# Order of filler work, of late products and of a few sums in a two-layer decoder kernel

## The chip, the cores and the metric

The kernel runs on one core of one Trainium2 chip. The metric is the time of one execution in microseconds (us). Three runs of the kernel before took 2700.45, 2702.9 and 2701.96 us, so the median is 2701.96 us.

The engines are named as the profile names them: PE is TensorE (matrix products, transposes), PEld its weight loads, DVE is VectorE, ACT is ScalarE, POOL is GpSimd, SP is SyncE, whose queue issues the transfers.

## The reference

Two layers run over 1024 tokens of 1024 features, all in fp32. Cut to what matters:

```python
for l in range(DEPTH):                       # 2
    h = rmsnorm(x, norm1[l])
    qa, ka, va, qb, kb, vb, gate_pre = jnp.split(h @ w_in[l], splits, axis=-1)
    o_a = dilated_mixture(qa, ka, va)        # 12 heads in 3 groups: window, dilation (128,1) (512,4) (2048,16)
    o_b = stick_breaking_attention(qb, kb, vb)   # 4 heads
    gates = sigmoid(gate_pre + b_gate[l]); g_a, g_b = gates[..., :D], gates[..., D:]
    x = x + (g_a * (o_a @ w_br[l, :256]) + g_b * (o_b @ w_br[l, 256:])) @ w_o[l]
    up = rmsnorm(x, norm2[l]) @ w_up[l]      # 1024 x 5632
    a, v = up[..., :2816], up[..., 2816:]
    a = causal_depthwise_conv(a, conv_w[l], conv_b[l])      # 3 taps
    x = x + (gelu(a) * v) @ w_down[l]
out = rmsnorm(x, norm_f)
```

Stick-breaking attention takes, for a query and the keys before it, the sigmoid of a score times the product of one minus the sigmoids of all keys between.

## The kernel before

**Arithmetic.** Each fp32 operand of a product is split in two parts, `hi` (a cast by ACT, L129) and `lo` (the rest, a subtraction by DVE, L130). A product is three matrix products: hi with hi, hi with lo, lo with hi (`product`, L150 to L159; `seven`, L902 to L909). Large products are cut into blocks of which seven, instead of eight, are multiplied; the sums and differences of blocks that this needs are made by POOL and DVE.

**Who sets the order.** PE runs in the order in which the program is written (L1870). ACT, DVE, POOL and SP are put in order by a planner: among the pieces that are ready on its own clock it takes the one written earliest. `tc.high_priority(offset=AHEAD)`, AHEAD being 200, lets pieces count as if they had been written 200 instructions earlier. While FFN units from the third on are written (L1714), ACT, DVE and POOL too run in the written order; SP does not.

**The mixer.** The attention is a list of 36 items (L1203 to L1216): 16 of stick-breaking attention (B00 to B17, line names `z`, `beta`, `sb_t`, `sb_o`), four of the near group (N00 to N11: `z0`, `p0`, `t0`, `o0`), 16 of the two far groups (T00 to T17: `z10`, `p1`, `t1`, `o1`). The trace leaves digits at the end of names out. An item has *scores* (PE products into a bank of PSUM, then DVE and ACT) and pairs of a *turn* (PE transposes of the weights, then a split by ACT and DVE in `parts`, L593) and a *product* with the values. PE does nothing else between them than *filler steps* of the dense projections: keys, queries, values, gates (`k_ps`, `q_ps`, `v_ps`, `r_ps`, `i_a`, `i_c`). A step is six matrix products. `attend` (L312) writes this order: the scores of the next item among the turns and products of this one, each product one place behind the next turn; the last product of an item (`late`) goes behind the first turn of the next. `Dense.step` (L254) writes one filler step. `Dense.advance(rate)` (L285) also lets one prepared piece of block sums go (`aside`), and adds the rate to an account, `due`; each whole unit in it buys a step. The rates are 0.68, 0.85, 0.88 and 0.77 (L41). If the next item is not ready when the current one begins, its scores are left over: `attend` then runs the dense units on until it is, two steps more, and then the scores.

**The queries** (`queries_half`, L532) of the second stick-breaking pair and of the near items: a product into a bank with the tag `ps`, of which there are two, then two multiplies by ACT (L538), two copying transfers from SP (L540), and two subtractions by DVE (L543, L544). Only after the last one can a later unit have the bank.

**The FFN.** A unit j makes 128 columns of the gate half and of the value half; `gated` (L1373) multiplies them. Units are taken in pairs, an even and an odd one, for the seven-product form of the down projection: `less` (L1381) makes differences on POOL (L1382), and `spill` (L1404) splits a block and writes it to DRAM (`gd`). `at(k, f)` runs f k steps later. `C[0]`, the two blocks of unit 0, lies in a buffer with the tag `ql`, of which there are two; the raw weights of a later unit (`up_a`, L1493 to L1495) take the same tag. The turn of unit 1 comes while units 2 and 3 run.

The lines that choose where fillers and late products go:

```python
for f in sc:                      # the first item's scores, L323
    f()
    dense.advance(rate)
...
if m == 0 and late:               # L331
    seq.append(late)
...
if nxt:                           # scores left over, L369
    for f in nxt:
        f()
        dense.advance(rate)
```

Of the kernel before, what the change touches and what calls it, by code (L numbers as in the profile page):

```python
# [11 lines left out]
ALU = mybir.AluOpType  # L12
# [32 lines left out]
AHEAD = 200  # L45
# [7 lines left out]
def trunk_kernel(ctx, tc, x, norm1, w_in, b_gate, w_br, w_o, norm2, w_up, conv_w, conv_b, w_down, norm_f, out, depth=None, probe=None):  # L53
# [258 lines left out]
    def attend(dense, items):  # L312

        late = None
        for i, (name, first, rest, rate, make) in enumerate(items):
            if i == 0:
                dense.until(first)
                dense.step()  # L320
                dense.step()
                sc, micro = make()
                for f in sc:  # L323
                    f()
                    dense.advance(rate)
                dense.done.add(name + "s")
            dense.until(rest)
            seq = []
            for m, (t, p) in enumerate(micro):
                seq.append(t)  # L330
                if m == 0 and late:  # L331
                    seq.append(late)
                if m >= 1:
                    seq.append(micro[m - 1][1])

            def late(f=micro[-1][1], name=name):
                f()
                dense.done.add(name)

            nxt, nmicro = [], None  # L340
            pending = items[i + 1] if i + 1 < len(items) else None

            def begin():
                nonlocal pending, nxt, nmicro
                if pending and set(pending[1]) <= dense.done:
                    nxt, nmicro = pending[4]()
                    pending = None

            begin()
            if pending or i + 1 == len(items):  # L350
                seq.append(late)
                late = None
            gap = max(1.0, len(seq) * 0.7 / max(1, len(nxt)))
            at = 0.0
            for j, f in enumerate(seq):
                if nxt and j >= at:
                    nxt.pop(0)()
                    at += gap
                    if not nxt:
                        dense.done.add(items[i + 1][0] + "s")  # L360
                    dense.advance(rate)
                f()
                dense.advance(rate)
            if pending:
                dense.until(pending[1])
                dense.step()
                dense.step()
                begin()
            if nxt:  # L369
                for f in nxt:  # L370
                    f()
                    dense.advance(rate)
                dense.done.add(items[i + 1][0] + "s")
            micro = nmicro

    H = [[None, None], [None, None]]

    def h_part(n, k):
        return H[n][0][:, k, :], H[n][1][:, k, :]
# [150 lines left out]
        yield  # L530

    def queries_half(q, w, n, scale, copies=False):  # L532
        qt, ql = q
        o = bank("ps", "q_ps")
        yield from product(o, [(w[k], h_part(n, k)) for k in range(KD)])
        qa, qb, la, lb = (a[:, i, n * HF : (n + 1) * HF] for a in (qt, ql) for i in range(2))
        for q2, src, mine, other in ((qa, o[0:64], slice(0, 64), slice(64, 128)), (qb, o[64:128], slice(64, 128), slice(0, 64))):
            act.mul(q2[mine], src, scale)  # L538
            if copies:
                nc.sync.dma_start(f32(q2[other]), f32(q2[mine]))  # L540
            else:
                act.mul(q2[other], src, scale)
        dve.scalar_tensor_tensor(la[0:64], o[0:64], scale, f32(qa[0:64]), ALU.mult, ALU.subtract)  # L543
        dve.scalar_tensor_tensor(lb[64:128], o[64:128], scale, f32(qb[64:128]), ALU.mult, ALU.subtract)  # L544
        yield

    def new_q():

# [773 lines left out]
    def ffn(l, pending, final):  # L1322
# [50 lines left out]
        def gated(j, n, v):  # L1373


            c = C[j][n]
            dve.tensor_tensor(c, c, v, ALU.mult)  # L1377

            later = (2, 3, 4, 5, 7) if j == 1 else (3, 5, 7, 9, 11) if j == NF - 1 else (1, 4, 7, 11, 14)

            def less(dst, a, b):  # L1381
                return lambda: pool.tensor_tensor(dst, a, b, ALU.subtract)  # L1382

            if j % 2 == 0:
                c11, c12 = C[j]
                if n == 0:
                    at(3, lambda: spill(j, 0, c11))
                else:
                    at(4, less(c11, c12, c11))
                    at(6, lambda: spill(j, 5, c11))  # L1390
            elif n == 1:
                s1, c12 = C[j - 1]
                c21 = C[j][0]
                at(1, less(c12, c, c12))
                at(1, less(s1, c, s1))
                at(later[0], lambda: spill(j, 6, c))
                at(later[1], lambda: spill(j, 2, c12))

                at(later[1], less(c, c21, s1))
                at(later[2], lambda: spill(j, 1, s1))  # L1400
                at(later[3], lambda: spill(j, 4, c21))
                at(later[4], lambda: spill(j, 3, c))

# [493 lines left out]
```

## Time and profile before

| what | value |
|---|---|
| median of three runs | 2701.96 us |
| the profiled execution | 2703.52 us, of which the span from the first to the last instruction is 2701.8 us |
| granted TensorE clock, mean | 0.996 |
| PE busy | 98% of the span |
| DVE busy | 78% |
| ACT busy | 49% |
| POOL busy | 27% |

Layer 1's mixer takes about 72 to 575 us of the span (B items to 230, N items to 330, T items from 397 to 556), its FFN starts at 735; layer 2's mixer takes about 1410 to 1912 us.

How to read the rows: in a list of waits a row says which engine's instruction (line, tile) sat idle until which other engine's piece was done, then the total in us, the number of times, and the longest. In a timeline a row has the start, the duration, the engine, the line, the operation, what it writes and reads, the shapes and a count, and in square brackets how long the engine stood idle in front of it and for whom. In a table of stretches each engine has its busy time and a count, then comes the granted clock, the DMA share and GB/s.

### The profile page before, as it was taken

Reading aid. Unit: us, or ns where it says so; the run is one execution under the profiler, and the core shown is the slowest. Engines: PE = TensorE matmul, PEld = TensorE weight load, DVE = VectorE, ACT = ScalarE, POOL = GpSimd, SP = SyncE. Lnnn points to the kernel's source line nnn. Section 1 sums busy time; section 2 is a strip of 40 time slices with the busy share of each in tenths; the row PEclk is TensorE's granted clock in tenths of the full one; section 3 lists DMA queues with packets and bytes.
Section 4 is the critical chain, followed back from the end, with each engine's and each line's share of the span. In section 5 each row is a group of like instructions: output and inputs, shape, how many; then the busy total and the mean of one; then the engine's idle time right before and its main releaser. Section 6 shows DMA issues by size and latency. Waiting matters only on the chain. (4 is left out here: it accounts for less than half of the span.)

```text
span 2701.8 us, 37158 instructions
## 1 busy us (share of the span) xinstructions
PE 2650.5 (98%) x13098; PEld 2226.4 (82%) x13098; DVE 2115.7 (78%) x3170; ACT 1314.3 (49%) x2434; POOL 734.9 (27%) x531
## 2 busy tenths in 40 slices
PE   8999999999999999999999999999999999999999
PEld 7888888888888888888889878888788888888888
DVE  5888876675789988897658887766858888998865
ACT  5656544364455555432335655434635555554225
POOL 2004133222233434321120042332311433343210
PEclk9999999999999999999999999999999999999999
DMA  4134489863235444688401334988732443447963
GB/s 153 28 97 125 132 239 234 205 229 118 82 117 172 141 156 143 222 325 313 167 32 48 102 120 145 254 208 226 234 90 75 151 160 135 170 144 254 333 246 121
DMA packets 399559, 448.88 MB, mean 166 GB/s; under 512 B 22044, under 2 KB 319372, under 8 KB 397836
## 3 DMA queue, kind: packets, MB, share of 16 engines
q1 hardware_dynamic: 399372, 446.49, 51.9%
q8 instruction: 104, 1.70, 0.3%
q14 instruction: 83, 0.68, 0.1%
HBM read 300.61 MB, written 142.67 MB: 164 GB/s over the span
## 5 line engine op out<-in xcount | busy, mean ns | idle before, releaser
L130 DVE TENSOR_TENSOR w_lo<-up_a,w_hi 128x512 fp32r<-128x512 f32 x240 | 236.9, 993 | 22.5 <-ACT w_hi L129 22.5
L129 ACT CAST w_hi<-up_a 128x512 fp32r<-128x512 f32 x240 | 149.4, 623 | 186.0 <-PE u_a L906 45.8
L1651 DVE TENSOR_TENSOR x<-x,d_ps 128x512 f32<-128x512 f32 (+1 forms) x228 | 152.3, 672 | 78.0 <-PE d_ps L1645 77.0
L1382 POOL TENSOR_TENSOR cv<-cv 128x512 f32<-128x512 f32 x88 | 131.9, 1509 | 249.0 <-DVE cv L1377 139.1
L130 DVE TENSOR_TENSOR w_lo<-w_raw,w_hi 128x512 fp32r<-128x512 f32 x176 | 133.9, 763 | 64.9 <-ACT w_hi L129 62.3
L129 ACT CAST w_hi<-w_raw 128x512 fp32r<-128x512 f32 x176 | 109.1, 621 | 130.1 <-PE o_ps L156 60.2
L129 ACT CAST w_hi<-in_a 128x512 fp32r<-128x512 f32 x140 | 86.8, 620 | 148.8 <-PE i_a L906 83.4
L130 DVE TENSOR_TENSOR g<-cv,g 128x512 fp32r<-128x512 f32 x154 | 152.3, 990 | 5.2 <-ACT g L129 2.8
L1643 PE MATMUL d_ps<-gd_in,w_hi 128*128 128x512 f32 (+1 forms) x340 | 130.2, 383 | 1.5 <-ACT w_hi L129 1.2
L1645 PE MATMUL d_ps<-gd_in,w_lo 128*128 128x512 f32 (+1 forms) x340 | 129.8, 382 | 0.0
L1644 PE MATMUL d_ps<-gd_in,w_hi 128*128 128x512 f32 (+1 forms) x340 | 129.7, 382 | 0.0
L905 PE MATMUL u_a<-hh,w_hi 128*128 128x512 f32 x320 | 124.7, 390 | 2.7 <-DVE u L1533 2.7
L906 PE MATMUL u_a<-t_lo,w_hi 128*128 128x512 f32 x320 | 124.5, 389 | 0.0
L907 PE MATMUL u_a<-hh,w_lo 128*128 128x512 f32 x320 | 124.5, 389 | 0.0
L905 PE MATMUL u_a<-t_hi,w_hi 128*128 128x512 f32 x320 | 124.5, 389 | 0.0
L906 PE MATMUL u_a<-hl,w_hi 128*128 128x512 f32 x320 | 124.5, 389 | 0.0
L907 PE MATMUL u_a<-t_hi,w_lo 128*128 128x512 f32 x320 | 124.5, 389 | 0.0
L130 DVE TENSOR_TENSOR w_lo<-in_a,w_hi 128x512 fp32r<-128x512 f32 x140 | 115.6, 826 | 3.8 <-ACT w_hi L129 3.5
L1038 POOL TENSOR_TENSOR in_a<-in_a 128x512 f32<-128x512 f32 x28 | 38.0, 1357 | 281.3 <-DVE w_lo L130 281.3
L1643 PE MATMUL d_ps<-gd_in,wd 128*128 128x512 f32 (+1 forms) x292 | 113.9, 390 | 0.0
L129 ACT CAST g<-cv 128x512 fp32r<-128x512 f32 x154 | 94.9, 616 | 38.1 <-POOL cv L1382 29.3
L1645 PE MATMUL d_ps<-gd_in,wd 128*128 128x512 f32 (+1 forms) x292 | 112.8, 386 | 0.0
(395 smaller groups left out, 8706.3 us busy)
## 6 DMA issues: line engine op xcount, KB each, us to landing
gd<-g SPq DMA_DIRECT2D x154, 512.0 KB, 3.6
gd_in<-gd SPq DMA_DIRECT2D x154, 512.0 KB, 6.2
up_a<-in_w_up_dram SPq DMA_DIRECT2D x80, 512.0 KB, 5.7
in_a<-in_w_in_dram SPq DMA_DIRECT2D x56, 512.0 KB, 5.4
w_raw<-in_w_in_dram SPq DMA_DIRECT2D x104, 256.0 KB, 3.4
t_kq<-tk SPq DMA_DIRECT2D x64, 384.0 KB, 7.6
wd_raw<-in_w_down_dram SPq DMA_DIRECT2D x22, 1024.0 KB, 8.0
gin<-gs SPq DMA_DIRECT2D x32, 512.0 KB, 5.2
```

What stands on the lines that cost most here:

```text
L129: act.copy(hi, src)
L130: dve.tensor_tensor(lo, src, f32(hi), ALU.subtract)
L905: pe.matmul(o, w[0][:, c], rh, start=(first and i == 0), stop=False, skip_group_check=True)
L906: pe.matmul(o, w[0][:, c], rl, start=False, stop=False, skip_group_check=True)
L907: pe.matmul(o, w[1][:, c], rh, start=False, stop=(last and i == 3), skip_group_check=True)
L1038: pool.tensor_tensor(a11, a22, a11, ALU.subtract)
L1382: return lambda: pool.tensor_tensor(dst, a, b, ALU.subtract)
L1643: pe.matmul(o[:, sub], wh[:, c], gh[:, sub], start=(i == 0 and k in (0, 4, 5)), stop=False, skip_group_check=True)
L1644: pe.matmul(o[:, sub], wh[:, c], gl[:, sub], start=False, stop=False, skip_group_check=True)
L1645: pe.matmul(o[:, sub], wl[:, c], gh[:, sub], start=False, stop=(i == m - 1), skip_group_check=True)
L1651: dve.tensor_tensor(x, x, o[:, sub], ALU.add)
```

## The change

It has five parts.

1. `attend`: behind each of the first item's scores stands a whole filler step (`dense.step()`) instead of `dense.advance(rate)`. The account and the block sums are not touched there.
2. `attend`: in the second item of the list the late product of the first item goes in front of the first turn instead of behind it. Other items keep their order.
3. `attend`: where scores were left over and the next item is of another kind (B, N, T), one more filler step follows them.
4. `queries_half`: what follows the product moves into a function `query_parts`, and for the queries with copies it is written with priority AHEAD.
5. `gated`: for unit 1 the two differences on POOL and the two spills behind them change places, and the third difference is made by DVE, in front of both spills. For later odd units the list of steps is the same as before.

```diff
                 for f in sc:
                     f()
-                    dense.advance(rate)
+                    dense.step()
                 dense.done.add(name + "s")
...
                 if m == 0 and late:
-                    seq.append(late)
+                    seq.insert(0 if i == 1 else 1, late)
...
                 dense.done.add(items[i + 1][0] + "s")
+                if items[i + 1][0][0] != name[0]:
+                    dense.step()
...
     def queries_half(q, w, n, scale, copies=False):
-        qt, ql = q
         o = bank("ps", "q_ps")
         yield from product(o, [(w[k], h_part(n, k)) for k in range(KD)])
+        with tc.high_priority(offset=AHEAD if copies else 0):
+            query_parts(q, o, n, scale, copies)
+        yield
+
+    def query_parts(q, o, n, scale, copies):
+        qt, ql = q
         qa, qb, la, lb = (a[:, i, n * HF : (n + 1) * HF] for a in (qt, ql) for i in range(2))
...
-        yield
...
-            def less(dst, a, b):
-                return lambda: pool.tensor_tensor(dst, a, b, ALU.subtract)
+            def less(dst, a, b, eng=pool):
+                return lambda: eng.tensor_tensor(dst, a, b, ALU.subtract)
...
-                at(1, less(c12, c, c12))
-                at(1, less(s1, c, s1))
+                pairs = [(2, c12), (1, s1)]
+                if j == 1:
+                    pairs.reverse()
+                for _, t in pairs:
+                    at(1, less(t, c, t))
                 at(later[0], lambda: spill(j, 6, c))
-                at(later[1], lambda: spill(j, 2, c12))
-
-                at(later[1], less(c, c21, s1))
-                at(later[2], lambda: spill(j, 1, s1))
+                if j > 1:
+                    at(later[1], lambda: spill(j, *pairs[0]))
+                at(later[1], less(c, c21, s1, dve if j == 1 else pool))
+                if j == 1:
+                    at(later[1], lambda: spill(j, *pairs[0]))
+                at(later[2], lambda: spill(j, *pairs[1]))
                 at(later[3], lambda: spill(j, 4, c21))
```

## The prediction

> **What bounds the kernel now.** I read the page's first parts, then TensorE's list of waits, by layer, then the timeline around each wait.
>
> ```profile
> span 2701.8 us, 37158 instructions
> ...
> PE 2650.5 (98%) x13098; PEld 2226.4 (82%) x13098; DVE 2115.7 (78%) x3170; ACT 1314.3 (49%) x2434; POOL 734.9 (27%) x531
> ```
>
> TensorE is busy for 2650.5 of 2701.8 us. The diff adds and removes no matrix product, so all that it can move is TensorE's idle time, at most 51 us. The waits in the mixer, layer 1 (72 to 575 us of the span) and then layer 2 (1410 to 1912 us); the columns are total, number of times, longest:
>
> ```profile
> PE o L729 <- DVE p0l L130: 5.3, 4, 3.1
> PE z L590 <- DVE st L813: 1.5, 1, 1.5
> PE z L590 <- ACT beta L631: 1.4, 3, 0.6
> PE r_ps L155 <- DVE ql L544: 1.4, 1, 1.4
> PE sb_t L646 <- DVE beta L636: 1.3, 1, 1.3
> PE o L831 <- DVE p1l L130: 0.9, 1, 0.9
> PE sb_o L657 <- DVE sbl L130: 0.9, 2, 0.5
> PE z L590 <- DVE st L708: 0.6, 1, 0.6
> PE i_a L905 <- DVE u L1051: 0.6, 1, 0.6
> ```
>
> ```profile
> PE o L729 <- DVE p0l L130: 5.3, 4, 3.1
> PE z L590 <- ACT beta L631: 1.8, 3, 1.0
> PE z L590 <- DVE st L813: 1.7, 1, 1.7
> PE r_ps L155 <- DVE ql L544: 1.4, 1, 1.4
> PE sb_t L646 <- DVE beta L636: 1.3, 1, 1.3
> PE z L590 <- DVE st L708: 1.3, 1, 1.3
> PE o L831 <- ACT p1h L129: 1.2, 1, 1.2
> PE sb_o L657 <- DVE sbl L130: 0.7, 2, 0.4
> PE o L831 <- DVE p1l L130: 0.2, 1, 0.2
> ```
>
> The sums are 13.9 and 14.9 us. In the FFN one wait is within reach, over both layers:
>
> ```profile
> PE u_a L905 <- DVE u L1533: 2.7, 2, 1.6
> ```
>
> So 31.5 us are open to the change, in places of 0.4 to 3 us, each an attention step that comes to TensorE before VectorE or ScalarE is done.
>
> **Filler steps and their phase.** A filler step is six products of a projection:
>
> ```profile
> 77.19 0.40 PE L155 MATMUL k_ps<-hh,w_hi 128*128 128x512 f32 x1
> ...
> 78.57 0.27 PE L646 MATMUL sb_t<-ident,beta 128*128 128x128 f32 x1
> ```
>
> From 77.19 to 78.57 it is 1.4 us. Before, an account grows by the rate at each attention step, and a whole unit in it buys a filler. After the first two scores it stood at 1.36, so one filler came and 0.36 stayed. Now each of these scores gets a whole filler and the account stays at zero. The two orders of the opening, laid out from the code (s score, t turn, a product with the values, F filler, numbers for the items):
>
> ```
> before: s0 s0 F s1 F t0 s1 F s2 F t1 a0 F s2 F t1 a1 F
> after:  s0 F s0 F s1 t0 F s1 F s2 a0 F t1 F s2 t1 F a1 F
> ```
>
> *The opening.* Item 0's turn keeps one filler behind its last score instead of two. It does not wait now (the list has one sb_t wait per layer, and that is item 1's). The new wait lies between 0, if the chain is done anyway, and 1.4, the filler taken away; I take 0.5, nearer to 0, since the first score now starts a filler ahead of the second and their pieces no longer queue together on VectorE. Item 1's turn waits 1.3 now. The late product, moved in front of it, is work in that gap:
>
> ```profile
> 80.33 0.36 PE L657 MATMUL sb_o<-sbh,vb 128*128 128x256 f32 x1
> ...
> 80.83 0.45 PE L155 MATMUL k_ps<-hh,w_hi 128*128 128x512 f32 x1
> ```
>
> It takes 0.5, so 0.8 is left; the keys' halves that VectorE writes there now come a filler earlier, and I take 0.4 (0 to 0.8). The score's wait for a bank, 0.6 and 1.0, keeps its distance. Net: +0.5 -0.9 = -0.4 a layer, -0.8. The late product waits for nothing more, being two fillers behind its own turn.
>
> *The slide.* From there on each skipped filler falls elsewhere, since the account is 0.36 lower, in all items. By the two orders, the pairs that wait get one filler more in all four small places of the first attention (both sb_o, two of the three z behind beta): 0.9 + 0.8 and 0.7 + 0.8 go, -3.2. Six pairs of a turn and its product go from three fillers to two in each layer; of 17 with two before, two waited (0.9), so 6 x 0.9/17 = 0.3 a layer comes back: -2.6 in sum.
>
> In the near items, the third score of the first (waiting for st L708, 0.6 and 1.3) gets a filler more: -1.9. The 5.3 of each layer are four waits, two of them in one stretch where VectorE is behind:
>
> ```profile
> 265.68 1.45 DVE L130 TENSOR_TENSOR w_lo<-w_raw,w_hi 128x512 fp32r<-128x512 f32 x1
> ...
> 272.49 0.38 PE L729 MATMUL o<-p0l,v 128*128 128x256 f32 x1 [3.06 <-DVE p0l L130]
> ```
>
> The product at 272.49 gets one filler more (3.1 - 1.4 = 1.7 left); the one before it, 1.3, keeps its two; the other two, 0.9 together, get one more and go. So -2.3 a layer. Six other pairs fall to two fillers; outside that stretch six such pairs waited 0.9 together, 0.15 each; I take twice that, as two of the new ones lie beside the stretch: 0.3 x 6 = +1.8 a layer. Net -1.9 - 4.6 + 3.6 = -2.9.
>
> In the far items the two neighbouring scores without a filler between them (1.5 and 1.7) are the third and fourth; after, those get one and the ninth and tenth lose theirs: 0. The last product (0.9; 1.4) gets a filler more, and six pairs fall to one filler, where five before held that wait alone: I take 0.1 for each of the new ones, +1.3 in sum: -2.3 + 1.3 = -1.0, between -2.3 and, with a wait as long as the old one in each layer, 0.
>
> *The switch of kind.* The added step runs only where scores are left over behind an item. From the first kind to the second the new scores are used up inside the item, so it does nothing; from the second to the third it makes two fillers out of one in front of a score that does not wait: 0. Its other end is the tail, where up to two fillers fewer cover the way to the branch products:
>
> ```profile
> 1910.07 1.29 DVE L130 TENSOR_TENSOR ol_a<-on,oh_a 128x512 fp32r<-128x512 f32 x2
> ...
> 1916.14 0.39 PE L156 MATMUL br_ps<-ol_a,br_w 128*128 128x512 f32 x1
> ```
>
> VectorE is done at 1911.4, the product comes at 1916.1; two fillers are 2.8 of those 4.8 us, so 0. If that cover were gone, it would cost the rest of the 2.8.
>
> **The queries' parts.** The two multiplies of ScalarE end at 181.0; VectorE's two subtractions start 2.7 us later, behind scans:
>
> ```profile
> 179.79 1.21 ACT L538 ACTIVATE qt<-q_ps 64x512 fp32r<-64x512 f32 x2
> ...
> 180.46 1.28 DVE L634 TENSOR_TENSOR_SCAN stay<-stay,zero 128x512 f32<-128x512 f32 x1
> ...
> 184.34 0.69 DVE L544 SCALAR_TENSOR_TENSOR ql<-q_ps,qt 64x512 fp32r<-64x512 f32 x1
> ...
> 185.18 0.47 PE L155 MATMUL r_ps<-hh,w_hi 128*128 128x512 f32 x1 [1.36 <-DVE ql L544]
> ```
>
> With chain priority they go behind the scan that runs at 181.0, at 181.7, and end by 183.1, before r_ps wants the bank at 183.8. So 1.4 goes in each layer, -2.7. On VectorE, scans and multiplies queue up to 1.4 behind them, and on ScalarE other chain pieces 1.2; their turn waits for them. The bounds are -2.7 and +2.7 (the same 1.4 paid by a turn in each layer); I take the full gain, as by the order a filler of 1.4 lies between r_ps's start and the next turn. The copies' transfers move ahead on SP too, and a weight load queued behind one waits for ScalarE's 1.2 us; loads are fetched a unit ahead, four fillers of 1.4, so 0.
>
> **The FFN's sums.** Only unit 1 changes; for later units the list of steps comes out the same. The next weights use unit 0's buffer, which the two spills behind the sums free:
>
> ```profile
> 768.02 1.61 POOL L1382 TENSOR_TENSOR cv<-cv 128x512 f32<-128x512 f32 x1 [0.70 <-DVE g L130]
> ...
> 768.40 2.38 DVE L130 TENSOR_TENSOR g<-cv,g 128x512 fp32r<-128x512 f32 x2
> ...
> 770.84 1.25 SPq L1495 DMA_DIRECT2D up_a<-in_w_up_dram  x2
> ...
> 776.39 0.62 ACT L129 CAST w_hi<-up_a 128x512 fp32r<-128x512 f32 x1 [5.19 <-DMA up_a<-in_w_up_dram]
> ```
>
> The load is issued at 770.84, when the second g ends, and ScalarE waits for it. After, VectorE has the third subtraction in front of the two g. Beside GpSimd's 1.61 the two g took 2.38; two pieces of that size took 1.29 where GpSimd stood still (the ol_a row), so three take 1.94 and free the buffer 0.44 sooner: -0.9 in both layers. The bounds: a piece more and no speeding up is +0.65 a layer, +1.3; the whole wait is -2.7. I take the value by the ol_a row, which is of the same size and engine. [...]
>
> **The sum.** -0.8 -2.6 -2.9 -1.0 -2.7 -0.9 = -10.9. ScalarE's, VectorE's, GpSimd's and SP's queues are planned anew from the changed order, outside the FFN's units, and a stall like that of 272.49 (six lower-priority pieces in front of p0l) can come up anew; I add one such, +3.1, for both layers together (bounds -3 and +9). That gives -7.8. The profiled execution took 2703.5 with its 1.7 outside the span; the median of the runs, 2702.0, is 1.5 under it. From the median: 2694.2, taken as 2694.
>
> **The rivals.**
>
> *The waits only change place.* Most shortened pairs wait as much as the lengthened ones did. For it: the far items' skip, which moves from one pair of scores to another at the same price. Against it: r_ps, the FFN and the first near item have a cover of their own. Then only -2.7, -0.9 and the +3.1 stay: 2701.5.
>
> *Slower: the shortened pairs wait more.* Ten pairs in the first attention, 7 near and 13 far ones lose a filler or a step of their cover in each layer, 60 in all. At 0.4 each that is +24. The parts above give, without what I let come back, -0.8 -3.2 -1.9 -4.6 -2.3 -2.7 -0.9 = -16.4. So +7.6, 2709.6; the point from which it costs time is 16.4/60 = 0.27 a pair. For it: the eight near pairs with two fillers waited 5.3, 0.66 each, the bad stretch among them. Against it: only two of 17 waited in the first attention, one of five in the far items.
>
> *A stall that costs clock.* The stretch at 265 to 272 has the longest mixer wait, and the clock held; the kernel's start, with a wait of 5.2 us, shows less (a row of the list of waits, then two of a table of stretches):
>
> ```profile
> PE x_t L1846 <- issue: 5.2, 1, 5.2
> ```
>
> ```profile
> 8.00:20.00 12.00, 6.83 (x40) 6.65 (x39) 10.52 (x22) 9.03 (x19) 0.00 (x0) 0.57 0.79 268
> 265.00:272.00 7.00, 3.61 (x17) 2.76 (x17) 6.97 (x10) 3.92 (x8) 3.19 (x2) 1.00 0.19 56
> ```
>
> If the second queries' subtractions (1.4) land in front of p0l there, that wait stays at 3.1 instead of 1.7, and a little more queueing would bring it nearer to the first row's case. Seven microseconds at 0.57 lose 3.0; with the 1.4 that is 4.4 a layer: +8.8 on 2694, 2703. [...]
>
> **Chances and range.** Forecast 0.5 (its own range 2688 to 2697), waits change place 0.31, slower by pairs 0.12, clock 0.07. A measurement here can tell about 0.2%, 5.4 us: faster is under 2696.6, slower over 2707.4. Faster: the forecast, plus a little of the second: 0.52. Slower: 0.13. Same: 0.35. The range reaches from 2686 (the -10.9 with no new stall, and 5 more of the listed waits gone) to 2706, which leaves the worse half of the slower case out.
>
> **What would show it.** Right: r_ps no longer waits for ql L544; sb_t for beta falls from 1.3 to under 0.5; st L708 goes; the wait of o L729 at 272.49 falls from 3.1 to about 1.7, and the group to 4.8 a layer; the wait for st L813 is at the ninth and tenth far items; up_a is issued 0.4 sooner and u_a waits 2.7 - 0.9 = 1.8 in all. Wrong: o L729 over 5.3 or new sb_t waits in most items (slower pairs), a granted clock under 1 around 265 us, or a wait of the branch products for ol_a.

## The result

The changed kernel is slower. Five runs took 2711.25 to 2719.05 us, median 2712.36; five of the kernel before, on the same chip, 2700.08 to 2705.14, median 2701.96. The ratio is 1.0043, with an interval of 1.0032 to 1.0055: +10.4 us where 8 fewer were forecast, and above the range of 2686 to 2706.

The profiled execution took 2712.22 us. The head of its page:

```profile
span 2710.4 us, 37117 instructions
...
PE 2660.6 (98%) x13098; PEld 2229.9 (82%) x13098; DVE 2113.5 (78%) x3172; ACT 1314.1 (48%) x2434; POOL 734.9 (27%) x529
```

TensorE issues the same 13098 products as before, and its idle time, summed up to its last product, *fell*, from 45.8 to 44.3 us. (1.1 of these 1.5 lie in the first 60 us, where TensorE waits for the first transfers and the change does nothing; behind them the sum went from 36.7 to 36.3.) Its busy time rose by 10.1. So the time did not go where the prediction looked. Rows of the list of TensorE's waits in the mixer, layer 1 (total, times, longest):

```profile
PE r_ps L155 <- DVE ql L551: 3.8, 2, 2.5
PE o L735 <- ACT p0h L129: 3.1, 2, 1.6
PE z L596 <- DVE st L819: 1.9, 1, 1.9
PE r_ps L155 <- DVE v L520: 1.1, 1, 1.1
PE sb_t L652 <- DVE beta L642: 0.9, 2, 0.5
PE o L735 <- DVE p0l L130: 0.6, 2, 0.3
```

Layer 2:

```profile
PE r_ps L155 <- DVE ql L551: 5.0, 2, 3.7
PE z L596 <- DVE st L819: 2.8, 1, 2.8
PE o L735 <- ACT p0h L129: 1.6, 1, 1.6
PE sb_t L652 <- DVE beta L642: 0.6, 2, 0.4
PE o L735 <- DVE p0l L130: 0.6, 2, 0.3
PE z L596 <- DVE st L714: 0.2, 1, 0.2
```

Against the two lists of before: the 5.3 of `p0l` is down to 0.6, the waits for `st` of the near items (0.6 and 1.3) to nothing and 0.2, `sb_t` is down, and in their place stand waits of 1.5 to 3.7 us for `ql`, for `p0h` and, longer than before, for the far items' scores. And the clock drops behind them. Rows of a table of stretches, in pairs: a stretch of 3.41 us with a wait in it, and the next 3.41 us. The columns are the limits, the length, the busy time of PE, PEld, DVE, ACT and POOL with counts, the granted clock, the DMA share and GB/s:

```profile
272.45:275.86 3.41, 0.94 (x7) 0.60 (x6) 3.37 (x5) 1.58 (x3) 0.46 (x1) 1.00 0.10 24
275.86:279.27 3.41, 3.41 (x12) 2.84 (x11) 3.41 (x7) 0.00 (x0) 0.00 (x0) 0.50 0.57 186
...
1832.34:1835.75 3.41, 1.49 (x10) 1.36 (x11) 3.01 (x9) 1.50 (x5) 2.66 (x2) 1.00 0.56 156
1835.75:1839.16 3.41, 3.41 (x11) 2.73 (x10) 0.61 (x2) 1.70 (x5) 0.00 (x0) 0.50 1.04 216
```

In the second row of each pair the granted clock is 0.50, and 11 or 12 products are done where the same 3.41 us of the kernel before, from 275.86, hold 21. There are six such stretches between 60 us and the end (from 265.62, 275.86, 490.90, 1600.23, 1620.71 and 1835.75), where the trace of before has two (421.20 and 1759.23). By estimate each costs 3.41 x 0.5 = 1.7 us where TensorE has work all through it. (At the very start, where TensorE waits for transfers, the clock is halved in some executions and not in others; the opening takes 73.7 us in before with 10.24 us of it and 73.0 in the changed kernel without any, so it is not counted.)

So of the 8.6 us between the spans, four more half-clock stretches are +6.8 and the idle time -1.5. The remaining 3.3 us are slower steps of TensorE that I did not settle.

By stage, in us, from the first instruction of a group on TensorE to that of the next (length, and in it idle time; n is the number of half-clock stretches), layer 1 / layer 2:

| stage | before | after |
|---|---|---|
| B items (`sb_t` to the first near turn) | 169.1, 5.6 / 170.0, 6.5 | 169.2, 4.9 / 169.0, 4.7 |
| N items (to the first `i_a`) | 77.6, 4.3 / 77.6, 4.4 | 82.1, 6.2, n 2 / 82.1, 5.9, n 2 |
| T items (first `t_kq` score to `br_ps`) | 176.5, 3.1, n 1 / 176.6, 3.2, n 1 | 178.6, 4.1, n 1 / 176.7, 3.3, n 1 |
| FFN up (`u_ps` to `d_ps`) | 429.2, 1.9 / 429.6, 2.4 | 429.0, 1.3 / 429.2, 1.9 |

The near items take 4.5 us more in each layer. The far items of layer 1 take 2.1 more, half of it idle time; the rest nearly balances.

**The stretch that the prediction looked at.** Rows of the timeline, VectorE, then TensorE:

```profile
268.48 3.28 DVE L943 TENSOR_TENSOR h_sum<-hh,h_sum 128x512 f32<-128x512 f32 x2
271.68 1.78 DVE L944 TENSOR_TENSOR h_sum<-h_sum,hl 128x512 f32<-128x512 f32 x1
273.38 0.68 DVE L130 TENSOR_TENSOR w_lo<-w_raw,w_hi 128x512 fp32r<-128x512 f32 x1
273.99 0.67 DVE L550 SCALAR_TENSOR_TENSOR ql<-q_ps,qt 64x512 fp32r<-64x512 f32 x1
274.67 0.69 DVE L551 SCALAR_TENSOR_TENSOR ql<-q_ps,qt 64x512 fp32r<-64x512 f32 x1
...
275.51 0.47 PE L155 MATMUL r_ps<-hh,w_hi 128*128 128x512 f32 x1 [2.47 <-DVE ql L551]
...
271.29 1.62 POOL L1043 TENSOR_TENSOR in_a<-in_a 128x512 f32<-128x512 f32 x1
```

In before GpSimd's sums of the first `in_a` block ran from 263.17 to 268.26 and slowed the `t_lo` and `w_lo` pieces beside them, one of which the prediction quoted; `p0l` was late. Two rows of the timeline of before, two `t_lo` pieces that took 1.37 us together in e10_before_dve (below), and a sum beside them:

```profile
263.01 2.43 DVE L130 TENSOR_TENSOR t_lo<-h_sum,t_hi 128x512 fp32r<-128x512 f32 x2
...
264.97 1.61 POOL L1034 TENSOR_TENSOR in_a<-in_a 128x512 f32<-128x512 f32 x1
```

Now the same sums run from 268.23 to 272.91, beside two `h_sum` pieces (3.28 us, 1.28 in before) and a third (1.78, 0.68 in before), and the last queries' `ql` is late instead. TensorE's `r_ps` needs the bank that `ql` frees.

### The profile page after: what moved, and what is told of

Read it like the earlier page. It is cut to its first block, busy times and chain, and to the rows that moved or that the text cites. A ratio compares the mean times of both kernels' runs of the same rounds, so it can differ in the third digit from the quotient of the medians.

```text
span 2710.4 us, 37117 instructions
## 1 busy us (share of the span) xinstructions
PE 2660.6 (98%) x13098; PEld 2229.9 (82%) x13098; DVE 2113.5 (78%) x3172; ACT 1314.1 (48%) x2434; POOL 734.9 (27%) x529
## 5 line engine op out<-in xcount | busy, mean ns | idle before, releaser
L1654 PE MATMUL d_ps<-gd_in,wd 128*128 128x512 f32 (+1 forms) x292 | 113.9, 390 | 0.0
L130 DVE TENSOR_TENSOR w_lo<-in_a,w_hi 128x512 fp32r<-128x512 f32 x140 | 109.7, 785 | 4.4 <-ACT w_hi L129 3.9
L1656 PE MATMUL d_ps<-gd_in,wd 128*128 128x512 f32 (+1 forms) x292 | 112.8, 386 | 0.0
L1655 PE MATMUL d_ps<-gd_in,wd 128*128 128x512 f32 (+1 forms) x292 | 112.8, 386 | 0.0
```

What stands on the lines that cost most here:

```text
L130: dve.tensor_tensor(lo, src, f32(hi), ALU.subtract)
L1654: pe.matmul(o[:, sub], wh[:, c], gh[:, sub], start=(i == 0 and k in (0, 4, 5)), stop=False, skip_group_check=True)
L1655: pe.matmul(o[:, sub], wh[:, c], gl[:, sub], start=False, stop=False, skip_group_check=True)
L1656: pe.matmul(o[:, sub], wl[:, c], gh[:, sub], start=False, stop=(i == m - 1), skip_group_check=True)
```

## The experiments

All kernels were timed beside the kernel before, with 4 to 12 runs each; its median lay between 2701.1 and 2702.1 in every group. Span, idle time and lists come from one execution of each kernel, which need not be a typical one: that of e15_late was the shortest of its 12 runs (2695.4 us), that of e13_after_kept the longest (2710.0). `idle` is TensorE's idle time in the profiled execution, `n` the half-clock stretches of 3.41 us between 60 us and the end.

| kernel | median, us | ratio to before, interval | span | idle | n |
|---|---|---|---|---|---|
| before | 2702.0 | | 2701.8 | 45.8 | 2 |
| after | 2712.4 | 1.0043, 1.0032 to 1.0055 | 2710.4 | 44.3 | 6 |
| e1_opening | 2727.2 | 1.0091, 1.0077 to 1.0104 | 2726.3 | 56.3 | 9 |
| e2_queries | 2703.7 | 1.0009, 1.0001 to 1.0018 | 2705.4 | 45.4 | 5 |
| e3_ffn | 2702.2 | 1.0004, 0.9995 to 1.0013 | 2698.7 | 42.2 | 2 |
| e4_no_queries | 2722.8 | 1.0082, 1.0068 to 1.0096 | 2720.5 | 53.1 | 7 |
| e5_opening_kept | 2703.4 | 1.0009, 1.0000 to 1.0018 | 2700.3 | 42.9 | 3 |
| e6_slide | 2721.2 | 1.0073, 1.0061 to 1.0086 | 2719.3 | 53.8 | 6 |
| e7_lead | 2720.6 | 1.0069, 1.0056 to 1.0083 | 2718.9 | 52.6 | 8 |
| e8_switch | 2705.3 | 1.0009, 0.9999 to 1.0019 | 2703.6 | 43.6 | 3 |
| e9_before_nosums | 2693.8 | 0.9975, 0.9965 to 0.9985 | 2692.7 | 36.8 | 1 |
| e10_before_dve | 2693.5 | 0.9970, 0.9960 to 0.9980 | 2691.8 | 34.8 | 2 |
| e11_opening_nosums | 2711.2 | 1.0044, 1.0031 to 1.0057 | 2709.3 | 49.2 | 2 |
| e12_after_dve | 2713.5 | 1.0048, 1.0035 to 1.0061 | 2709.5 | 45.2 | 4 |
| e13_after_kept | 2705.8 | 1.0011, 1.0003 to 1.0020 | 2708.3 | 47.1 | 5 |
| e14_after_kept_dve | 2697.5 | 0.9983, 0.9975 to 0.9992 | 2693.8 | 36.7 | 2 |
| e15_late | 2701.6 | 0.9993, 0.9985 to 1.0002 | 2693.6 | 38.2 | 2 |
| e16_best | 2696.9 | 0.9978, 0.9970 to 0.9986 | 2694.3 | 38.2 | 1 |
| e17_fill | 2722.0 | 1.0068, 1.0054 to 1.0081 | 2722.6 | 50.3 | 6 |
| e18_dve_late | 2693.4 | 0.9969, 0.9959 to 0.9980 | 2695.5 | 37.2 | 3 |

Take idle and n x 1.7 off the span, and between 2651.5 and 2657.5 is left in every row (in e17_fill too, once its 5.5 us of added products are taken off). Waits and half-clock stretches account for the differences to within about 3 us.

**Which part? Four kernels with one part, or all but one.**

```diff
 e1_opening: part 1 alone
-                    dense.advance(rate)
+                    dense.step()
```

> Only the filler steps behind the first two scores (part 1), the rest as before, so the account runs 0.36 lower from there on. The changed kernel took 10.4 us more than the kernel before (2712.4 against 2702.0); its trace has 1.5 us less idle time of TensorE but six 3.41-us stretches at half clock between 100 and 2600 us where before had two (about 1.7 us lost in each), four of them within 12 us of the waits of o for p0h L735 and of r_ps for ql L551. Theory slide (the shifted skips make these waits): this kernel has them too and takes about 2710, at least +6. Theory queries (the parts put ahead make them): about 2700, -2, with half-clock stretches at two places as before. My prediction's terms for this part alone gave about -7 to -9.

```diff
 e2_queries: part 4 alone
+        with tc.high_priority(offset=AHEAD if copies else 0):
+            query_parts(q, o, n, scale, copies)
```

> Only the chain priority of the queries' parts (part 4). Theory queries: the p0h and r_ps stalls around 255 to 276 and 1600 to 1620 us come with it, 5 to 7 us of waits and four half-clock stretches, about +8 (2710). Theory slide: without the shifted skips the stalls stay away, and r_ps's wait of 1.4 a layer stays or goes: -3 to 0. The prediction's term was -2.7.

```diff
 e3_ffn: part 5 alone
-                at(later[1], less(c, c21, s1))
+                at(later[1], less(c, c21, s1, dve if j == 1 else pool))
...
```

> Only the order of unit 1's sums in the FFN (part 5). All theories: the waits of u_a in the unit behind go from 2.7 to between 1.1 and 1.8 in both layers together, nothing else moves, -1 to -1.6 us, within what the runs can tell (0.2%).

```diff
 e4_no_queries: parts 1, 2, 3 and 5
-        with tc.high_priority(offset=AHEAD if copies else 0):
```

> The changed kernel with the queries' parts as before (parts 1, 2, 3 and 5). Theory queries: the four half-clock stretches and the waits for p0h and ql around 255 to 276 and 1600 to 1620 go, about 2700 (-12 against the changed kernel). Theory slide: they stay, 2709 to 2712.

The theory that blames the queries' parts falls: alone they cost 2, and without them the rest of the change is 10 us worse than with them. One line, part 1, costs 26 us alone; the theory of the slide had about 8 for it, and for e4_no_queries too it came out 11 us too low. TensorE's longest wait in layer 1, from the list of waits of e1_opening:

```profile
PE r_ps L155 <- DVE ql L544: 6.7, 2, 4.7
```

The same of e4_no_queries:

```profile
PE r_ps L155 <- DVE ql L546: 6.6, 2, 4.7
```

And two rows of that list of e2_queries:

```profile
PE o L733 <- DVE p0l L130: 6.7, 5, 2.9
PE r_ps L155 <- DVE ql L549: 0.9, 1, 0.9
```

With the slide, the priority takes the longest wait for `ql` from 4.7 to 2.5 us; without it, `ql` gains 0.5 and the `p0l` behind it loses 1.4 (6.7 for 5.3). The FFN's part is worth no time that the runs can tell. In e3_ffn two rows of the list are left of the 2.7 us that `u_a` waited:

```profile
PE u_a L905 <- DVE u L1538: 0.7, 1, 0.7
PE u_a L905 <- ACT u L1521: 0.6, 1, 0.6
```

But in e8_switch, where the FFN is that of before, the row is

```profile
PE u_a L907 <- DVE u L1535: 4.0, 2, 2.1
```

and in e15_late, with the same FFN, there is none. Over the 13 traces without part 5 all waits of `u_a` come to 0 to 4.0 us, 2.1 on average; over the seven with it, to 1.3 to 3.0, 2.1 on average. So one trace against another shows no gain here.

**What in part 1? The opening, the place of the skips, or the lead.**

```diff
 e5_opening_kept: two steps, account as if none had been added
-                    dense.advance(rate)
+                    dense.step()
+                dense.due += 2 * rate - 2
```

> The two filler steps behind the first scores, but the account is set to -0.64 behind them, so that from the next step on every filler of TensorE stands where it stood before. Theory slide (part 1 costs 26 us in e1_opening because the skipped fillers fall elsewhere): about 2700, -2 to 0, with the kernel before's waits behind the opening and the opening's sb_t wait changed only. Theory opening (the changed opening plans the other engines' queues anew, and those make the stalls): 2710 or more, with r_ps waiting over 4 us for ql L544 as in e1_opening.

```diff
 e6_slide: opening as before, account 0.36 lower
                     dense.advance(rate)
+                dense.due -= 0.36
```

> The opening as before, and 0.36 taken off the account behind the first two scores: the skips fall where they fall in the changed kernel, each filler at the same place or one later than in before. Theory slide by the place of the skips: the same stalls as in e1_opening, 2720 or more. Theory slide by the fillers' lead (in e1_opening 0.64 of a filler more is out on average; here 0.36 fewer): other stalls than in e1_opening, the r_ps wait under 2 us; time anywhere between 2698 and 2710. Theory opening: 2702.

```diff
 e7_lead: two steps, skips where they were
-                    dense.advance(rate)
+                    dense.step()
+                dense.due += 0.36
```

> The two filler steps, and 0.36 left on the account: the skips fall at the same steps as before, but exactly one filler more is out all along. Theory slide by the place of the skips: 2699 to 2703, as e5_opening_kept. Theory slide by the lead (the last products of the queries and the first with the sums come one filler earlier against the attention's pieces, GpSimd's sums and SP's loads): stalls again in the near items around 255 to 285 us, r_ps waiting over 3 us for ql, 2712 to 2730.

```diff
 e8_switch: part 3 alone
+                if items[i + 1][0][0] != name[0]:
+                    dense.step()
```

> Only the added step at the switch of kind (part 3). The prediction's term was 0, between 0 and +2.8 a layer in the tail. Theory lead: the far items run one filler ahead and get new waits there, +2 to +6; no change ahead of 400 us and between 1410 and 1750 us of the span.

The opening itself is harmless (e5_opening_kept), which leaves the slide; and both ways of sliding cost the same 19 us, at different places. The longest group in the list of waits of layer 1, of e6_slide:

```profile
PE sb_t L647 <- DVE beta L637: 6.7, 4, 2.4
```

Of e7_lead:

```profile
PE r_ps L155 <- DVE ql L545: 7.7, 2, 5.0
```

And the two rows of that list by which e5_opening_kept differs from before (1.3 and 1.4 there):

```profile
PE sb_t L647 <- DVE beta L637: 2.2, 2, 1.7
PE z L591 <- ACT beta L632: 0.8, 2, 0.4
```

With 0.36 of a filler less (e6_slide) the turns of the stick-breaking items wait for `beta`, 6.7 in a layer instead of 1.3. With a whole filler more and every skip where it was (e7_lead) the r_ps units wait for `ql`, as in e1_opening. So neither the place of the skips nor the lead is the cause by itself (e6_slide has the time of the first of its theories, with waits that this theory did not have): of the four positions of the account that were run, the one of before is the cheapest by 19 us. e8_switch, which moves the far items' fillers by one, is within the bound.

**Is it the pile-up beside GpSimd?** The first `in_a` block's four sums were left out, or given to VectorE, for the kernel before and for kernels with the slide.

```diff
 e9_before_nosums (before) and e11_opening_nosums (e1_opening): first block of a layer
+            sums = hasattr(dense, "begun")
+            dense.begun = True
...
-            pool.tensor_tensor(a21, a21, a22, ALU.add)
+            if sums:
+                pool.tensor_tensor(a21, a21, a22, ALU.add)
...
 e10_before_dve (before) and e12_after_dve (after)
+            eng = dve if not hasattr(dense, "begun") else pool
+            dense.begun = True
...
-            pool.tensor_tensor(a21, a21, a22, ALU.add)
+            eng.tensor_tensor(a21, a21, a22, ALU.add)
```

> The kernel before with GpSimd's four sums on the first in_a block (L1031 to L1038, once per layer) left out, so that the gates made from that block are wrong and the time is that of less work. Theory pile-up beside GpSimd: these sums run from 263.2 to 268.3 and VectorE's t_lo and w_lo pieces beside them take 2.43, 1.45 and 2.37 instead of 1.28, 0.69 and 1.28 (3.0 us more) in front of the p0l that ends the waits of 1.28 and 3.06: both shrink to under 1.3 together, in both layers, -5 to -8 us (2693 to 2697). Rival, the order of the queues alone: the waits stay over 3 a layer and the time within 2 us of before.

> The kernel before with the same four sums made by VectorE instead of GpSimd, for the first in_a block only. Theory pile-up beside GpSimd: 3.0 us of slowing goes and up to 2.7 (four sums at 0.68) come, some of them behind the p0l that is waited for: -1 to -4 (2698 to 2701), the 3.06 wait under 2.5. Rival, VectorE's queue is full anyway: +1 to +5.

> The kernel of e1_opening (part 1 alone, 2727.2) with the same four sums of GpSimd left out (less work, the gates of that block are wrong). Theory pile-up beside GpSimd: h_sum, h_sum and w_lo in front of ql take 1.28, 0.68 and 0.68 instead of 2.39, 1.76 and 1.75, so ql ends 3.3 us sooner, the r_ps waits of 4.7 and 4.3 fall to about 1.2, and the half-clock stretches behind them go: 2713 to 2717. Rival, the lead alone (ql comes late because its product does): the waits stay over 3.5, 2722 or more.

> The changed kernel (2712.4) with the four sums made by VectorE. Theory pile-up beside GpSimd: h_sum at 3.28 for two and 1.78 for one go to 1.28 and 0.68, 3.1 us, against up to 2.7 for the sums themselves: the r_ps waits of 2.5 and 3.7 shrink by 0.5 to 3, and where a half-clock stretch goes with them 1.7 more each: 2704 to 2711. Rival, VectorE's queue is full anyway: 2712 to 2718.

Leaving the sums out is worth 7.3 us to the kernel before and 16 to e1_opening, whose wait for `ql` falls from 4.7 to 1.4 us with no half-clock stretch left beside it. VectorE's making them instead is worth 7.5 to the kernel before, more than the 1 to 4 expected. In e10_before_dve, the timeline shows what 2.43 + 1.45 + 2.37 us in before have become, and the wait that was 3.06:

```profile
261.83 1.37 DVE L130 TENSOR_TENSOR t_lo<-h_sum,t_hi 128x512 fp32r<-128x512 f32 x2
263.55 0.69 DVE L130 TENSOR_TENSOR w_lo<-w_raw,w_hi 128x512 fp32r<-128x512 f32 x1
...
268.51 0.38 PE L729 MATMUL o<-p0l,v 128*128 128x256 f32 x1 [1.33 <-DVE p0l L130]
```

So beside GpSimd's sums VectorE's pieces took 6.25 us, and 3.43 without them, and in the kernel before that decides: three sums of 1.6 to 1.7 us on GpSimd (the fourth runs much later) cost more as neighbours than as 0.68 us pieces in VectorE's own queue. But the pile-up is not what the change adds: without it e11_opening_nosums is still 17 us above e9_before_nosums, and e12_after_dve gains nothing on the changed kernel. There the waits for `ql` shrink (3.8 to 2.2 in layer 1), and a new one, for a sum behind the same pieces, takes their place, as the list of waits of e12_after_dve has it:

```profile
PE i_a L911 <- DVE u L1059: 2.3, 2, 1.8
PE r_ps L155 <- DVE ql L551: 2.2, 2, 1.4
```

**Is it the slide in the whole change, and what do the other parts give?**

```diff
 e13_after_kept: the changed kernel, account as before up to the last near item
                     dense.step()
+                dense.due += 2 * rate - 2
...
 e14_after_kept_dve: the same, with the four sums by VectorE
 e15_late: part 2 alone
 e16_best: e5_opening_kept, parts 2 and 5, the four sums by VectorE
 e18_dve_late: part 2 and the four sums by VectorE
```

> The changed kernel with the account set to -0.64 behind the first two scores, so that up to the last near item every filler stands where it stood in before; the other four parts stay. Theory slide: the 10.4 us go, 2698 to 2704; the waits of the changed kernel for p0h L735 and z for st L819 of 1.9 and 2.8 go, and r_ps waits under 2 a layer. Rival, the small parts add up (alone they gave +2.6, +1.1, +2.0 and +4.0 with medians inside or near the bound of the runs): 2709 to 2713.

> The kernel of e13_after_kept with the four sums of the first in_a block made by VectorE. Theory pile-up beside GpSimd: as from the kernel before to e10_before_dve, -7.5 against e13_after_kept, 2690 to 2697. Rival (the gain of e10_before_dve was particular to that order, as e12_after_dve with its +1 says): within 2 of e13_after_kept.

> Only the late product in front of the second item's turn (part 2). The prediction's term: the sb_t wait of 1.3 falls to about 0.4 to 0.8 in each layer, -0.9 to -1.8 in sum, nothing else moves: 2699 to 2701. Rival: the wait goes to the sb_o product itself or to the next turn: 2701 to 2703.

> The two opening steps with the account kept, the late product in front, the FFN's sums in the new order, and the four in_a sums by VectorE; no step at the switch and no priority for the queries' parts. If the gains add: e10_before_dve 2693.5, less 1 to 2 of waits in the opening, less 1 in the FFN: 2690 to 2692. If they do not: 2693 to 2697.

Taking only the slide out of the changed kernel brings the ratio from 1.0043 to 1.0011: 0.0032 x 2702 = 8.6 of the 10.4 us are the slide's, give or take about 4 by the two intervals. About 3 stay with the other parts. Part of it may be the priority of the queries' parts, whose `p0l` waits stand in layer 1 of e13_after_kept as they do in e2_queries; no run parts it from the added step at the switch, which alone gave as much (e2_queries and e8_switch, 1.0009 each). A far score waits 3.0 there; but such a wait is 1.5 in before and 0.6 in e15_late, whose far items have the same order. From the list of waits of e13_after_kept, layer 1:

```profile
PE z L597 <- DVE st L820: 3.0, 1, 3.0
PE o L736 <- DVE p0l L130: 6.7, 5, 2.9
```

The late product in front (e15_late) takes `sb_t` from 1.3 to 0.9 in each layer, and no other change of its list can be put down to it:

```profile
PE sb_t L646 <- DVE beta L636: 0.9, 1, 0.9
```

Where the slide is absent the sums by VectorE gain again (e14_after_kept_dve, -8.3 by the medians). e16_best lies between e14_after_kept_dve and e10_before_dve; its opening steps, late product and FFN order add nothing measurable to e10_before_dve.

**Waits or clock?**

```diff
 e17_fill: e1_opening, the eighth r_ps unit of a layer
                 nc.sync.dma_start(kept_product(key), t)
                 yield
+            dense.units = getattr(dense, "units", 0) + 1
+            if dense.units == 8:
+                for _ in product(o, [(w[k], h_part(1, k)) for k in range(4)]):
+                    pass
```

> The kernel of e1_opening (2727.2) with twelve matrix products done twice, once in each layer: in front of the product r_ps that waited 4.7 and 4.3 us for ql, the twelve products of the half product ahead of it are made again into the same bank (same result; 12 at 0.23, about 2.7 us of TensorE's work that falls into the wait). Theory clock: the idle time there falls to about 2 us, the two half-clock stretches of 6.83 us behind it (3.4 us lost in each layer) stay away, nothing else changes: -5 to -7, 2720 to 2722, although TensorE does 5.4 us more work. Rival (the waits themselves cost the time and the half clock is only a sign of them): 2726 to 2730.

> The kernel before with the four in_a sums by VectorE (e10_before_dve, 2693.5) and the late product in front of the second item's turn (e15_late, sb_t's wait 1.3 to 0.9 in each layer), nothing else. If both add: 2692 to 2693.5, the lowest of all. If not: 2694 to 2697 as e16_best.

The end of the wait in the timeline of e1_opening:

```profile
280.03 0.77 PE L155 MATMUL r_ps<-hh,w_hi 128*128 128x512 f32 x1 [4.67 <-DVE ql L544]
```

Two stretches of e1_opening, the last of the wait and the 7 us behind it:

```profile
277.00:280.03 3.03, 0.00 (x0) 0.03 (x1) 2.99 (x5) 0.00 (x0) 0.43 (x1) 0.75 0.24 67
280.03:287.00 6.97, 6.97 (x25) 5.81 (x26) 4.92 (x9) 1.23 (x3) 0.00 (x0) 0.62 0.34 104
```

The end of the wait in e17_fill:

```profile
280.24 0.47 PE L155 MATMUL r_ps<-hh,w_hi 128*128 128x512 f32 x1 [1.34 <-DVE ql L544]
```

And its two stretches:

```profile
277.00:280.20 3.20, 1.90 (x9) 1.24 (x7) 3.15 (x5) 0.62 (x1) 0.64 (x1) 1.00 0.21 60
280.24:287.20 6.96, 6.96 (x38) 5.92 (x39) 6.93 (x12) 2.21 (x4) 0.00 (x0) 1.00 0.33 107
```

`ql` comes at the same moment (the product starts at 280.24 instead of 280.03), but TensorE has worked through most of the wait, the clock stays at 1.00, and in the 7 us behind it 38 products are done instead of 25. The kernel is 5.2 us faster by the medians with 5.5 us *more* work on TensorE. The N items got 2.4 and 2.2 us shorter in the two layers although the wait's end did not move: about that much of the stall's price was the clock. (It is not exact: the waits for `p0h` in the same items changed too, by -1.7 in layer 1 and +1.6 in layer 2, and at other places two half-clock stretches came up and one more went, so that nine became six and not five.)

e10_before_dve and e18_dve_late, 2693.5 and 2693.4, are 0.3% faster than the kernel before; the late product adds nothing that can be told.

## Why the prediction was wrong

**"All that it can move is TensorE's idle time" failed.** That sentence bounded the whole sum, and it left out how long the products themselves take. The clock is a second account: four more half-clock stretches, +6.8. The prediction had it only as a rival, at 0.07 and around 265 us alone, by comparison with a wait of 5.2 us; waits of 1.6 to 2.8 stood in front of five of the six half-clock stretches of the changed kernel, and one of 3.7 in front of the sixth. Between the -7.8 of the forecast and the +8.6 of the two spans lie 16.4 us; 6.8 of them are the clock, 6.3 the idle time, which fell by 1.5 and not by 7.8, and 3.3 are the slower steps that stay open.

**The slide, -2.6, -2.9 and -1.0, failed in size and sign.** It was priced as a redistribution: 18 pairs in each layer lose a filler of cover, each to wait 0.05 to 0.3 on average, by the mean of pairs of which most had not waited. (The 1.3 of the far items, 12 pairs at 0.1, should have been 1.2.) e6_slide and e7_lead measured +19 for 0.36 fewer and one more filler, e1_opening +26, and in the whole change it is about 8.6. The rival "the shortened pairs wait more" set the point of no gain at 0.27 a pair and had the sign right, but not the form: the shortened pairs hardly wait, a few chains do (`beta`, `p0h`, `ql`), by 1.5 to 6 us each, and half-clock stretches follow (6 to 9 of them in these three kernels, 2 in before). Why the position of before is the best of the four no run shows; that rates and priorities had been fitted to it is my guess, and by it the waits in the list of before were a remnant. That the known waits would leave was right (`p0l`, `st`, the shift of the far items' to the ninth and tenth scores, 1.9 and 2.8); that few would come was not.

**The allowance of 3.1 for one new stall** had the right kind of event in the right stretch and too few of them: r_ps for `ql` is +2.4 in layer 1 and +3.6 in layer 2 over before, `p0h` +3.1 and +1.6.

**The queries' parts, -2.7, failed.** ScalarE was done at 179.54, but VectorE took the scan, its multiply and a `w_lo` first, and `ql` ended at 183.45; r_ps waited 1.37 at 183.60, as before. A priority moves only pieces that are ready; that on the planner's clock those three were ready first is the likely reason, which no run shows. The term's other bound, the same 1.4 paid by another chain in each layer, is what e2_queries shows (`p0l` 6.7 for 5.3). In company of the slide the part is worth 10 us; there `ql` is the chain that is late, and its longest wait falls from 4.7 to 2.5.

**The opening, -0.8:** right in sign, and the new wait of the first turn, 0.53 in layer 1 and 0.22 in layer 2, is near the 0.5 that was taken. The second turn's wait went, where 0.4 was to stay; the rest of the 0.9 and 0.6 of `sb_t` is a later turn's. But the late product does not do this by itself, as the term has it: the second turn still waits 0.9 with it alone (e15_late), 1.78 with part 1 alone (e1_opening) and 1.41 with both but the account kept (e13_after_kept). It goes only with all three: in the changed kernel a whole filler stands between the late product and that turn, in e13_after_kept none. **The switch, 0:** within the bound, 1.0009, from 0.9999 to 1.0019.

**The FFN, -0.9:** the first half of the mechanism was right, the second is not shown. The third subtraction and two `g` took 1.9 us on VectorE with GpSimd at rest, where 1.94 was estimated. From the timeline of the changed kernel:

```profile
774.59 0.68 DVE L1388 TENSOR_TENSOR cv<-cv 128x512 f32<-128x512 f32 x1
775.19 1.28 DVE L130 TENSOR_TENSOR g<-cv,g 128x512 fp32r<-128x512 f32 x2
776.50 1.29 SPq L1506 DMA_DIRECT2D up_a<-in_w_up_dram  x2
```

The load is issued 56.4 us behind the FFN's first product (`u_ps`) in both layers of all seven kernels with part 5, and 56.9 to 57.0 in all 13 without it: 0.55 sooner, where 0.44 was forecast. In the changed kernel `u_a` waits 1.6 in all, for the 2.7 of before and the 1.8 forecast. That match is luck: when ScalarE comes to cast the loaded weights varies in layer 1 from 61.4 to 63.5 us behind `u_ps` without part 5 and from 61.1 to 62.6 with it, and the waits of `u_a` in both layers, 2.1 us on average with and without it, vary with it. The term took the issue alone to set that time.

## What to carry to other kernels

Where an account, a rate or a counter places filler work, a change of its phase is not a local edit: it moves everything behind it against the other engines' queues, here by 19 to 26 us at each of three other phases. Price it by running the phase alone (one line) before the parts that it comes with, and keep the phase when the edit is meant to be local (e5_opening_kept). Here 1.5 to 1.75 us of TensorE's idle time in one stretch were followed by half clock in 9 of 28 cases, and under 1.25 us in 13 of 15,236 (the table below); by estimate each costs 1.7 more, so few long waits and many short ones of the same sum were not the same price. Nor was the idle engine free: in the kernel before, three sums of 0.68 us in VectorE's full queue beat the same three at 1.6 on GpSimd, beside which two `t_lo` pieces of VectorE took 2.43 us instead of 1.37; in the changed kernel the move gained nothing. And a wait that stands in one trace may be another in the next (`u_a`): see how much it varies among kernels that don't touch it before putting a price on it.

## What the runs showed that was not expected

**The half-clock stretches lie on a grid of 3.413 us.** In every trace their starts lie whole multiples of 3.413 us apart (in the changed kernel 275.86 - 265.62 is 3.00 of them, 1600.23 - 265.62 is 391.0; in before 1759.23 - 421.20 is 392.0), and the offset differs between executions (the first limit of the grid lies at 1.36 us of the span in before, at 2.79 in the changed kernel). The length of a single gap does not tell where they come: none follows the one of 3.06 us in before, while gaps of 1.6 to 2.8 us in the changed kernel have one behind them. The table counts them by the idle time of TensorE summed inside the stretch ahead, over the 20 traces, with that grid laid over the idle times:

| idle time in a stretch, us | followed by half clock | of |
|---|---|---|
| 2.0 and more | 25 | 25 |
| 1.75 to 2.0 | 23 | 29 |
| 1.5 to 1.75 | 9 | 28 |
| 1.25 to 1.5 | 9 | 87 |
| under 1.25 | 13 | 15,236 |

**The same stall had half clock behind it in some traces and not in others.** The wait of about 3 us for `p0l` in the near items stands alike in both layers of six traces (before, e2, e3, e5, e8, e15), twelve times: six times no half-clock stretch follows, five times one, once two. The wait and the 7 us behind it in a table of stretches of the kernel before:

```profile
269.10:272.50 3.40, 0.34 (x3) 0.02 (x2) 3.40 (x7) 1.10 (x2) 0.00 (x0) 1.00 0.25 77
272.50:279.30 6.80, 6.80 (x37) 5.75 (x38) 6.71 (x12) 2.27 (x4) 0.00 (x0) 1.00 0.43 133
```

The same of e5_opening_kept:

```profile
268.00:271.42 3.42, 1.06 (x6) 0.61 (x4) 3.42 (x7) 1.13 (x3) 0.00 (x0) 1.00 0.37 113
271.42:278.25 6.83, 6.11 (x17) 4.97 (x18) 6.67 (x12) 0.54 (x2) 0.00 (x0) 0.50 0.42 136
```

In before a limit of the grid at 271.02 parts the wait into 1.6 and 1.5 us, and the clock stays at 1.00. In e5_opening_kept 2.4 us of it lie in one stretch, the half clock follows, and in the 6.8 us behind it 17 products are done where before has 37. That the kernel before held its clock there, on which the prediction rested, I put down to luck, since in six of the twelve cases it did not hold. Where a stall falls on the grid may be part of why the runs of one kernel differ (2698 to 2711 us for the kernel before); their times alone don't show it.
